# A hybrid decoder layer on one core: sine tables kept off other work, RG-LRU in finer steps and a later S5 scan, and smaller first transfers

## The chip, the cores and the metric

The kernel runs on one core of a Trainium2 chip. The core has a matrix engine (PE, with its weight loads as PEld), a vector engine (DVE), a scalar engine (ACT), a small general engine (POOL) and a sync engine (SP) that here issues nearly all transfers from memory. Each engine works through its own list of instructions in order and waits at semaphores for the others. The metric is device time in microseconds (us) of one execution; lower is better.

## The reference

One decoder layer on 256 tokens of width 2048, all in float32. The normed input is multiplied by one wide matrix; its columns feed three branches and three gates.

```python
xn = rms_norm(h, norm_mix_g)
proj = xn @ w_in                       # 2048 x 11264: u_s5, u_lru, q, k, v, gate_logits
gates = sigmoid(gate_logits + b_gate)
y_s5 = s5_branch(u_s5, ...)            # complex diagonal linear scan over time, gelu, glu
y_lru = rglru_branch(u_lru, ...)       # causal conv of 4 taps, two gates, real linear scan
y_attn = stick_breaking_attention(q, k, v)   # 8 heads, exp/log and a cumulative sum
merged = g_s5*(y_s5 @ w_br_s5) + g_lru*(y_lru @ w_br_lru) + g_attn*(y_attn @ w_br_attn)
h = h + merged @ w_out
h = h + squared_relu_mlp(rms_norm(h, norm_mlp_g), w_up, w_down)   # width 8192
return rms_norm(h, final_norm_g)
```

In the S5 branch the state turns by a fixed angle each step. The kernel takes the turning out before a real scan and puts it back after it, for which it needs, for each of eight blocks of channels, a table of cosines and sines of step times angle.

## The kernel before

**Weight units.** All large weights come in units of 256 x 512 values (512 KB), 520 of them, in one fixed list `stream`. Unit n passes through four hands. SP loads `raw_n` (`load_next`, L130). ACT casts it to a rounded half `hi_n` (`split_next`, L146). DVE subtracts, `lo_n` = `raw_n` - `hi_n` (L147). PE then multiplies: hi by the rounded activations, hi by their rest, and lo by the rounded ones, in three matmuls per tile, so that float32 is nearly kept. `chunk` (L225 to L227) does it with 24 matmuls of 128x256 per unit, `chunk_tok` (L241 to L243) with 12 of 128x512. raw, hi and lo have three buffers each: `hi_n` can be written only when PE has finished unit n-3, and `raw_n` is asked for only when `lo_(n-3)` is done.

**Units in order.** 0 to 15 give the RG-LRU input, 16 to 31 the S5 input. 32 to 79 are the RG-LRU gate and its branch product in turns of 8 and 4. 80 to 127 are k, q, v twice (four heads each time). 128 to 175 are the attention gate and branch in turns of 8 and 4 (gate: 128 to 135, 140 to 147, 152 to 159, 164 to 171), 176 to 191 the S5 gate's first half, and then come the S5 tail, the output product and the MLP.

**Side work.** Everything else (norm, RG-LRU, S5 scan, attention, gelu) is written as generators: pieces of work with `yield` between them. `later(gens, rate)` puts a generator in a list; after each unit's matmuls `pump` runs, on average, `rate` pieces of each generator in the list. So the rate and the number of yields say at which unit a piece is issued; then the framework's scheduler orders each engine's list. Side work on DVE and ACT thus stands between two lo's or two hi's, and whatever stands there delays the next one.

**The pieces that matter here.** `lru_half` runs the conv for a pair of channel tiles: one scaled copy on ACT (L535) and three multiply-adds on DVE (L537), then a yield; after that two sigmoid matmuls and sigmoids (L545, L546), Tanh, Exp, Sqrt, and a scan (L570) with the split of its result (L572, L573). It is queue `lq`, rate 1.15. The bank scalings of S5's input are L386. `s5_scan` (rate 1.27) starts as soon as its parameters are there: `s5_tables` makes a block's angles (L604), reduces them (L606, L607), takes Abs (L609) and two Sin on ACT (L610, L611), then `s5_split` and `s5_stack` build the scan's input with twelve 64 KB transfers on SP per block. Per block there follow six products on DVE (L660 to L670), eight scans (L705), six products (L681 to L692) and a sum into `us5` (L700). The next block's tables are stepped by hand between those products (`next(more, None)`). `gelu` has a Tanh, `gates` two multiply-adds on DVE (L750) and two Sigmoids on ACT (L751), `branch` the products with the gates (L760, or L762 and L763), `attention` per head Abs, Exp, Ln (L796 to L798), a suffix sum on PE and a last Exp (L811), all in a chain of seven steps. ACT holds one set of function tables at a time; where the set changes the list has an ACT_TABLE_LOAD.

**The start.** SP asks for x's tiles 0 and 1 in one transfer (256 KB), unit 0 in two, x's next pair, unit 1, and so on. The rounded x (`xhi`, L322) is made in `before_split` ahead of each unit's cast. Twenty small matmuls on ones keep PE busy from the start until the first unit is there.

Of the kernel before, what the change touches and what calls it, by code (L numbers as in the profile page):

```python
# [14 lines left out]
P = 128  # L15
L = 256
# [30 lines left out]
def hybrid_block(ctx: ExitStack, tc: tile.TileContext, io, out):  # L47
# [62 lines left out]
    st = {"load": 0, "split": 0, "use": 0}  # L110

    def pieces(i):
        return [slice(k, k + 1) for k in range(UK)] if i == 0 else [slice(0, UK)]

    def load_x(q):
        if q < KT // UK:
            s = slice(q * UK, q * UK + UK)
            nc.sync.dma_start(xT[:, s, :], io["x"][:, s, :])
        if q == 0:
            nc.scalar.dma_start(par, io["par"])  # L120

    def load_next():
# [6 lines left out]
        for k in pieces(i):  # L129
            nc.sync.dma_start(t[:, k, :], io[name][c * (ngrp[name] // (P * UK)) + g][:, k, :])  # L130
        raw[i] = t

    def split_next():
        i = st["split"]
        if i >= len(stream):
            return
        st["split"] += 1
        h = whi.tile([P, UK, CH], F32R, tag="hi", name=f"hi{i}")
        l_ = whi.tile([P, UK, CH], F32R, tag="lo", name=f"lo{i}")
        r = raw.pop(i)  # L140
        x = anchor.pop("x", None)
        es = ExitStack()
        if i == 0:
            es.enter_context(tc.issue_after(x))
        for k in pieces(i):
            anchor["act"] = nc.scalar.copy(h[:, k, :], r[:, k, :]).ins  # L146
            anchor["dve"] = nc.vector.tensor_tensor(l_[:, k, :], r[:, k, :], h[:, k, :].bitcast(F32), ALU.subtract).ins  # L147
        es.close()
        hi[i] = h, l_
# [82 lines left out]
    def chunk_tok(name, c, k, xs, hold=0, done=None):  # L232
# [12 lines left out]
        for g in range(ng - hold):  # L245
# [5 lines left out]
            anchor["pe"] = mm.ins  # L251
            pump()
# [47 lines left out]
    for q in range(3):  # L300
        load_next()
        load_x(q + 1)
# [220 lines left out]
    def lru_half(c, us):  # L523
# [9 lines left out]
        for u, cts, xc, r, i_, th in parts:  # L533
            for j, k in cts:
                nc.scalar.activation(xc[:, j, :], u[:, j, :], AF.Identity, scale=cw[:, 3, k], bias=cb[:, k])  # L535
                for s in range(1, 4):
                    nc.vector.scalar_tensor_tensor(xc[:, j, s:], u[:, j, :L - s], cw[:, 3 - s, k], xc[:, j, s:], ALU.mult, ALU.add)  # L537
                yield
# [37 lines left out]
    lq = later([lru_params()], 1.15)  # L576
# [16 lines left out]
    S5_RATE = 1.27  # L593

    def s5_tables(b):
# [7 lines left out]
        def gen():  # L603
            nc.vector.tensor_tensor(c, fhi[:, q, :].unsqueeze(3).broadcast_to(sh), flo[:, q, :].unsqueeze(2).broadcast_to(sh), ALU.add)  # L604
            yield
            nc.scalar.activation(sf, cf, AF.Identity, bias=magic)  # L606
            nc.vector.scalar_tensor_tensor(sf, sf, -MAGIC, cf, ALU.add, ALU.subtract)  # L607
            yield
            nc.scalar.activation(cf, sf, AF.Abs)  # L609
            nc.scalar.activation(sf, sf, AF.Sin, scale=-TURN)  # L610
# [20 lines left out]
    def s5_scan():  # L631
        v = ypool.tile([P, 2, NT, L], F32, tag="yhi", name="s5_v")
        t12 = ypool.tile([P, 2, NT, L], F32, tag="ylo", name="s5_t")
        vr, vi, t1, t2 = v[:, 0], v[:, 1], t12[:, 0], t12[:, 1]
        tabs, more = s5_tables(0)
        yield from more
        s5_split(0)
# [6 lines left out]
        for b in range(WT):  # L644
            c, s = tabs
# [9 lines left out]
            more = iter(())  # L655
            if b + 1 < WT:
                s5_split(b + 1)
                tabs, more = s5_tables(b + 1)
                yield
# [11 lines left out]
            next(more, None)  # L671
# [8 lines left out]
            next(more, None)  # L680
# [3 lines left out]
            next(more, None)  # L684
# [18 lines left out]

    def tt_scan(o, r, i):
        nc.vector.tensor_tensor_scan(o, r, i, 0.0, ALU.mult, ALU.add)  # L705

    def gelu(b):
# [4 lines left out]
        yield  # L712
        nc.scalar.activation(g1, g1, AF.Tanh, scale=GELU_C * GELU_K)
# [21 lines left out]
    def gates(idx, c, alloc):  # L735
# [9 lines left out]
        later([bias()], 1.0)  # L745
        banks = chunk_tok("w_in", GATE0 + 4 * idx + c, D, xs)
        gts = []
# [37 lines left out]
    def attention(hs, kT, qT, vt):  # L785
# [27 lines left out]
        tc.keep_in_program_order(nc.scalar.preload_act_table_set("natural_log_exp_and_others"))  # L813
        yield
        for i in range(7):
# [4 lines left out]
            yield  # L820
        while vt[0] is None:
            yield
# [348 lines left out]
```

## Time and profile before

| what | value |
| --- | --- |
| time, three runs | 1508.52, 1511.49, 1511.58 us; median 1511.49 |
| profiled execution, time | 1512.1 us |
| its span | 1510.3 us |
| PE busy | 1488.4 us, 99% |
| DVE busy | 1175.2 us, 78% |
| ACT busy | 782.3 us, 52% |
| transfers, mean | 194 GB/s |

How the lines are read: a line of a timeline gives the start, the length, the engine, the line of the kernel, the operation, what it writes and reads, how many are taken together, and in brackets how long the engine had been idle and what ended that. Lengths of neighbours on one engine overlap a little (a lo of 1.22 us is followed by the next start 1.13 later), so pitches are taken from starts. A row of the view by windows has, for a stretch of time, the busy time and number of instructions of PE, PEld, DVE, ACT and POOL, then the granted clock of PE (1.00 is full), the share of the transfer engines, and GB/s. Times are in us from the start of the profiled execution's span.

### The profile page before, as it was taken

Reading aid. Unit: us, or ns where it says so; the run is one execution under the profiler, and the core shown is the slowest. Engines: PE = TensorE matmul, PEld = TensorE weight load, DVE = VectorE, ACT = ScalarE, POOL = GpSimd, SP = SyncE. Lnnn points to the kernel's source line nnn. Section 1 sums busy time; section 2 is a strip of 40 time slices with the busy share of each in tenths; the row PEclk is TensorE's granted clock in tenths of the full one; section 3 lists DMA queues with packets and bytes.
Section 4 is the critical chain, followed back from the end, with each engine's and each line's share of the span. In section 5 each row is a group of like instructions: output and inputs, shape, how many; then the busy total and the mean of one; then the engine's idle time right before and its main releaser. Section 6 shows DMA issues by size and latency. Waiting matters only on the chain.

```text
span 1510.3 us, 19900 instructions
## 1 busy us (share of the span) xinstructions
PE 1488.4 (99%) x7518; PEld 1260.5 (83%) x7518; DVE 1175.2 (78%) x1468; ACT 782.3 (52%) x920; POOL 35.3 (2%) x60
## 2 busy tenths in 40 slices
PE   9999999999999999999999999999999999999997
PEld 9997788989887878988887888888888888888886
DVE  6767998897988989689799796568854787558965
ACT  6767556565765564544455544344433444344443
POOL 1400000000000000000000000000000000000011
PEclk9999999999999999999999999999999999999999
DMA  9546766665555666666855666666666666666664
GB/s 287 157 153 176 228 205 201 187 182 168 175 172 183 208 182 210 189 202 190 276 182 188 197 184 205 194 185 196 198 194 193 193 195 195 195 191 191 192 197 152
DMA packets 89858, 292.41 MB, mean 194 GB/s; under 512 B 12834, under 2 KB 17058, under 8 KB 89634
## 3 DMA queue, kind: packets, MB, share of 16 engines
q1 hardware_dynamic: 89618, 291.07, 62.6%
q8 instruction: 59, 0.97, 0.3%
q14 instruction: 37, 0.30, 0.1%
q10 hardware_dynamic: 144, 0.07, 0.0%
HBM read 282.71 MB, written 2.10 MB: 189 GB/s over the span
## 4 chain that ended last, share of the span: by engine, by line
PE 83%; DVE 9%; issue 3%; ACT 2%; DMA 2%; SPq 0%; DVEq 0%; ACTq 0%
PE mt_w_up L242 6%; PE mt_w_up L241 6%; PE mt_w_up L243 6%; PE mt_w_in L242 5%; PE mt_w_in L243 5%; PE mt_w_in L241 5%; PE mt_w_down L242 4%; PE mt_w_down L241 4%; PE mt_w_down L243 4%; PE mp_w_down L277 4%; PE mp_w_down L278 4%; PE mp_w_down L276 4%; PE mm_w_in L227 4%; PE mm_w_in L225 4%; PE mm_w_in L226 4%; DVE lo L147 3%
## 5 line engine op out<-in xcount | busy, mean ns | idle before, releaser
L146 ACT CAST hi<-raw 128x1024 fp32r<-128x1024 f32 (+1 forms) x521 | 545.2, 1049 | 625.9 <-PE mt_w_up L243 131.4
L147 DVE TENSOR_TENSOR lo<-raw,hi 128x1024 fp32r<-128x1024 f32 (+1 forms) x521 | 637.9, 1225 | 287.7 <-ACT hi L146 284.1
L242 PE MATMUL mt_w_in<-lo,xhi 128*128 128x512 f32 x448 | 176.1, 393 | 3.9 <-DVE lo L147 3.7
L241 PE MATMUL mt_w_in<-hi,xhi 128*128 128x512 f32 x448 | 175.2, 396 | 0.2 <-ACT hi L146 0.2
L243 PE MATMUL mt_w_in<-hi,xlo 128*128 128x512 f32 x448 | 175.2, 391 | 0.0
L241 PE MATMUL mt_w_up<-hi,hhi 128*128 128x512 f32 x448 | 174.3, 389 | 0.0
L242 PE MATMUL mt_w_up<-lo,hhi 128*128 128x512 f32 x448 | 174.3, 389 | 0.0
L243 PE MATMUL mt_w_up<-hi,hlo 128*128 128x512 f32 x448 | 174.3, 389 | 0.0
L227 PE MATMUL mm_w_in<-xhi,lo 128*128 128x256 f32 x512 | 145.4, 286 | 4.5 <-DVE lo L147 4.5
L225 PE MATMUL mm_w_in<-xhi,hi 128*128 128x256 f32 x512 | 146.5, 286 | 0.5 <-ACT hi L146 0.4
L226 PE MATMUL mm_w_in<-xlo,hi 128*128 128x256 f32 x512 | 145.7, 285 | 0.0
L728 DVE STREAM_TRANSPOSE reluT<-relu 32x256 f32<-32x256 f32 x256 | 111.5, 436 | 4.2
L242 PEld LDWEIGHTS mt_w_in<-lo,xhi 128*128 128x128 f32 x448 | 84.6, 189 | 24.0 <-DVE lo L147 7.6
L227 PEld LDWEIGHTS mm_w_in<-xhi,lo 128*128 128x128 f32 x512 | 98.7, 194 | 5.5 <-DVE lo L147 5.5
L242 PE MATMUL mt_w_down<-lo,hd_hi 128*128 128x512 f32 (+1 forms) x272 | 102.5, 377 | 0.0
L241 PE MATMUL mt_w_down<-hi,hd_hi 128*128 128x512 f32 (+1 forms) x272 | 102.4, 377 | 0.0
L243 PE MATMUL mt_w_down<-hi,hd_lo 128*128 128x512 f32 (+1 forms) x272 | 102.4, 376 | 0.0
L225 PEld LDWEIGHTS mm_w_in<-xhi,hi 128*128 128x128 f32 x512 | 99.2, 194 | 1.1 <-ACT hi L146 1.0
L277 PE MATMUL mp_w_down<-lo,hd_hi 128*128 128x512 f32 x256 | 99.8, 390 | 0.1
L278 PE MATMUL mp_w_down<-hi,hd_lo 128*128 128x512 f32 x256 | 99.6, 389 | 0.0
L276 PE MATMUL mp_w_down<-hi,hd_hi 128*128 128x512 f32 x256 | 99.6, 389 | 0.0
L241 PEld LDWEIGHTS mt_w_in<-hi,xhi 128*128 128x128 f32 x448 | 84.5, 189 | 17.8 <-ACT hi L146 0.7
(299 smaller groups left out, 2370.2 us busy)
## 6 DMA issues: line engine op xcount, KB each, us to landing
raw<-in_w_in SPq DMA_DIRECT2D x175, 512.0 KB, 4.3
raw<-in_w_up SPq DMA_DIRECT2D x128, 512.0 KB, 4.2
raw<-in_w_down SPq DMA_DIRECT2D x128, 512.0 KB, 4.2
raw<-in_w_out SPq DMA_DIRECT2D x32, 512.0 KB, 4.2
raw<-in_w_br_lru SPq DMA_DIRECT2D x16, 512.0 KB, 4.6
raw<-in_w_br_attn SPq DMA_DIRECT2D x16, 512.0 KB, 4.1
raw<-in_w_br_s SPq DMA_DIRECT2D x16, 512.0 KB, 4.1
stk<-ux SPq DMA_DIRECT2D x96, 64.0 KB, 4.1
```

Of the source, the lines that this page charges most:

```text
L146: anchor["act"] = nc.scalar.copy(h[:, k, :], r[:, k, :]).ins
L147: anchor["dve"] = nc.vector.tensor_tensor(l_[:, k, :], r[:, k, :], h[:, k, :].bitcast(F32), ALU.subtract).ins
L225: nc.tensor.matmul(o, wh[:, kk, s], xh, start=first and ct % 2 == 0, stop=False, skip_group_check=True)
L226: nc.tensor.matmul(o, wh[:, kk, s], xl, start=False, stop=False, skip_group_check=True)
L227: mm = nc.tensor.matmul(o, wl[:, kk, s], xh, start=False, stop=last and ct % 2 == 1, skip_group_check=True)
L241: nc.tensor.matmul(banks[j], xh[:, s], wh[:, a:b], start=kt == 0, stop=False)
L242: nc.tensor.matmul(banks[j], xh[:, s], wl[:, a:b], start=False, stop=False)
L243: return nc.tensor.matmul(banks[j], xl[:, s], wh[:, a:b], start=False, stop=kt == ng * UK - 1)
L276: nc.tensor.matmul(o, xh[:, s], wh[:, kk, :], start=kt == 0, stop=False)
L277: nc.tensor.matmul(o, xh[:, s], wl[:, kk, :], start=False, stop=False)
L278: mm = nc.tensor.matmul(o, xl[:, s], wh[:, kk, :], start=False, stop=kt == ng * UK - 1)
L728: nc.vector.transpose(d_[32 * a:32 * a + 32, :, :, 32 * b:32 * b + 32], s_[32 * b:32 * b + 32, :, :, 32 * a:32 * a + 32])
```

## The change

- **Start.** x's first pair is asked for in two transfers of 128 KB, and unit 0, in pieces of a quarter, a quarter and a half, is asked for between the two. Its casts and subtractions have the same pieces.
- **RG-LRU.** The conv yields inside each channel tile too (after the second multiply-add), and the queue's rate goes from 1.15 to 1.45.
- **S5 scan.** It yields eight times before its first table, and its rate goes from 1.27 to 1.35. The tables' generator has more yields and becomes a task of its own (`later([chain_of(3, more)], S5_RATE)`), finished at the latest when its block begins, in place of being stepped by hand.
- **Sines, gelu's Tanh.** The two Sin of a table wait (by yielding) while `st["chain"]` is set, that is while an attention's seven steps run, and while `st["gate"]` is set with fewer than three units of a gate product left. Gelu's Tanh waits for `chain`.

```diff
     def pieces(i):
-        return [slice(k, k + 1) for k in range(UK)] if i == 0 else [slice(0, UK)]
+        if i == 0:
+            return [(slice(0, 1), slice(0, L)), (slice(0, 1), slice(L, CH)), (slice(1, 2), slice(0, CH))]
+        return [(slice(0, UK), slice(0, CH))]
...
         if q < KT // UK:
-            s = slice(q * UK, q * UK + UK)
-            nc.sync.dma_start(xT[:, s, :], io["x"][:, s, :])
+            for s in ([slice(k, k + 1) for k in range(UK)] if q == 0 else [slice(q * UK, q * UK + UK)]):
+                nc.sync.dma_start(xT[:, s, :], io["x"][:, s, :])
+                if q == 0 and s.start == 0:
+                    load_next()
...
             anchor["pe"] = mm.ins
+            st["left"] = ng - 1 - g
             pump()
...
                 for s in range(1, 4):
                     nc.vector.scalar_tensor_tensor(xc[:, j, s:], u[:, j, :L - s], cw[:, 3 - s, k], xc[:, j, s:], ALU.mult, ALU.add)
+                    if s == 2:
+                        yield
                 yield
...
-    lq = later([lru_params()], 1.15)
+    lq = later([lru_params()], 1.45)
...
-    S5_RATE = 1.27
+    S5_RATE = 1.35
...
             nc.vector.tensor_tensor(c, fhi[:, q, :].unsqueeze(3).broadcast_to(sh), flo[:, q, :].unsqueeze(2).broadcast_to(sh), ALU.add)
             yield
+            yield
             nc.scalar.activation(sf, cf, AF.Identity, bias=magic)
             nc.vector.scalar_tensor_tensor(sf, sf, -MAGIC, cf, ALU.add, ALU.subtract)
             yield
+            yield
             nc.scalar.activation(cf, sf, AF.Abs)
+            yield
+            while st["chain"] or st["gate"] and st["left"] < 3:
+                yield
             nc.scalar.activation(sf, sf, AF.Sin, scale=-TURN)
             nc.scalar.activation(cf, cf, AF.Sin, scale=-TURN, bias=half_pi)
             yield
...
+        for _ in range(8):
+            yield
         tabs, more = s5_tables(0)
         yield from more
+        more = None
...
         for b in range(WT):
+            if more is not None:
+                finish(more)
...
                 tabs, more = s5_tables(b + 1)
+                more = later([chain_of(3, more)], S5_RATE)
                 yield
...
+    def chain_of(n, gen):
+        for _ in range(n):
+            yield
+        yield from gen
...
         yield
+        while st["chain"]:
+            yield
         nc.scalar.activation(g1, g1, AF.Tanh, scale=GELU_C * GELU_K)
...
+        st["gate"] = True
         banks = chunk_tok("w_in", GATE0 + 4 * idx + c, D, xs)
+        st["gate"] = False
...
+        st["chain"] = True
         yield
         for i in range(7):
...
+        st["chain"] = False
         while vt[0] is None:
             yield
```

Where instructions land is shown at three places. The first is DVE around unit 26 (before: L537 is the conv, L386 the scaling of a finished S5 bank, L573 the rest of the RG-LRU result; in the changed kernel the same are L543, L392 and L581). Before:

```order
L147 TENSOR_TENSOR lo25_1082<-raw25_1034,hi25_1081 128x1024
L573 TENSOR_TENSOR ylru_lo_151<-lru_tc0_631,ylru_hi_150 128x512
L537 SCALAR_TENSOR_TENSOR lru_xc1_1069<-ulru2_817,par_79,lru_xc1_1069 128x255 x2
L537 SCALAR_TENSOR_TENSOR lru_xc1_1069<-ulru2_817,par_79,lru_xc1_1069 128x254 x2
L537 SCALAR_TENSOR_TENSOR lru_xc1_1069<-ulru2_817,par_79,lru_xc1_1069 128x253 x2
L386 TENSOR_TENSOR us5_99<-mm_w_in_0_0_16_821,rstd_135 128x512
L386 TENSOR_TENSOR us5_99<-mm_w_in_0_1_16_822,rstd_135 128x512
L147 TENSOR_TENSOR lo26_1120<-raw26_1079,hi26_1119 128x1024
```

The same place in the changed kernel:

```order
L151 TENSOR_TENSOR lo25_1076<-raw25_1038,hi25_1075 128x1024
L581 TENSOR_TENSOR ylru_lo_153<-lru_tc0_635,ylru_hi_152 128x512
L543 SCALAR_TENSOR_TENSOR lru_xc1_1103<-ulru2_801,par_79,lru_xc1_1103 128x255
L392 TENSOR_TENSOR us5_101<-mm_w_in_0_0_16_805,rstd_137 128x512
L543 SCALAR_TENSOR_TENSOR lru_xc1_1103<-ulru2_801,par_79,lru_xc1_1103 128x254
L392 TENSOR_TENSOR us5_101<-mm_w_in_0_1_16_806,rstd_137 128x512
L151 TENSOR_TENSOR lo26_1119<-raw26_1073,hi26_1118 128x1024
L543 SCALAR_TENSOR_TENSOR lru_xc1_1103<-ulru2_801,par_79,lru_xc1_1103 128x253
```

Four of the six conv steps have moved behind lo26. At lo14 likewise one conv step stands ahead in place of six.

The second is ACT around unit 131, in the second attention (L811 and L835 are the last Exp of a head, z6 and z7 its scores; ts5 and tc5 are the sine and cosine table of S5's sixth block). Before:

```order
L146 CAST hi130_4172<-raw130_4138 128x1024
L606 ACTIVATE ts5_3854<-tc5_3853,magic_133 128x1024
L811 ACTIVATE z7_4075<-z7_4075 128x384
L146 CAST hi131_4194<-raw131_4170 128x1024
L609 ACTIVATE tc5_3853<-ts5_3854 128x1024
L610 ACT_TABLE_LOAD
L610 ACTIVATE ts5_3854<-ts5_3854 128x1024
L611 ACTIVATE tc5_3853<-tc5_3853,half_pi_131 128x1024
L146 CAST hi132_4216<-raw132_4192 128x1024
```

In the changed kernel:

```order
L150 CAST hi130_4176<-raw130_4139 128x1024
L835 ACTIVATE z6_4025<-z6_4025 128x384
L623 ACT_TABLE_LOAD
L623 ACTIVATE ts5_3940<-ts5_3940 128x1024
L835 ACT_TABLE_LOAD
L835 ACTIVATE z7_4063<-z7_4063 128x384
L624 ACT_TABLE_LOAD
L624 ACTIVATE tc5_3939<-tc5_3939,half_pi_133 128x1024
L150 CAST hi131_4197<-raw131_4174 128x1024
L150 CAST hi132_4217<-raw132_4195 128x1024
```

The sines have moved from between hi131 and hi132 to between hi130 and hi131, with z7's Exp between them. At unit 151 it is the other way: before, the gate's table load and two Sigmoids stood between the two Sin of ts6 and tc6, and now the Sin stand ahead of hi147 and the Sigmoids alone ahead of hi151.

The third is SP at the start. Before:

```order
L118 DMA xT_81<-in_x 128x512
L130 DMA raw0_86<-in_w_in 128x512 x2
L118 DMA xT_81<-in_x 128x512
L130 DMA raw1_90<-in_w_in 128x1024
L118 DMA xT_81<-in_x 128x512
L130 DMA raw2_93<-in_w_in 128x1024
```

In the changed kernel:

```order
L120 DMA xT_81<-in_x 128x256
L134 DMA raw0_85<-in_w_in 128x256 x2
L134 DMA raw0_85<-in_w_in 128x512
L120 DMA xT_81<-in_x 128x256
L120 DMA xT_81<-in_x 128x512
L134 DMA raw1_92<-in_w_in 128x1024
L120 DMA xT_81<-in_x 128x512
L134 DMA raw2_95<-in_w_in 128x1024
```

x's second tile has moved behind all of unit 0, and raw1 from fifth to seventh place. On ACT the two casts of xhi still stand together ahead of the first piece of hi0.

More of the change, by code (lines that the diff above doesn't have):

```diff
@@ L109, in hybrid_block @@
     raw, hi, anchor = {}, {}, {}
-    st = {"load": 0, "split": 0, "use": 0}
+    st = {"load": 0, "split": 0, "use": 0, "gate": False, "left": 0, "chain": False}
     def pieces(i):
-        return [slice(k, k + 1) for k in range(UK)] if i == 0 else [slice(0, UK)]
+        if i == 0:
+            return [(slice(0, 1), slice(0, L)), (slice(0, 1), slice(L, CH)), (slice(1, 2), slice(0, CH))]
+        return [(slice(0, UK), slice(0, CH))]
     def load_x(q):
         if q < KT // UK:
-            s = slice(q * UK, q * UK + UK)
-            nc.sync.dma_start(xT[:, s, :], io["x"][:, s, :])
+            for s in ([slice(k, k + 1) for k in range(UK)] if q == 0 else [slice(q * UK, q * UK + UK)]):
+                nc.sync.dma_start(xT[:, s, :], io["x"][:, s, :])
+                if q == 0 and s.start == 0:
+                    load_next()
         if q == 0:
@@ L128, in load_next @@
         t = wraw.tile([P, UK, CH], F32, tag="raw", name=f"raw{i}")
-        for k in pieces(i):
-            nc.sync.dma_start(t[:, k, :], io[name][c * (ngrp[name] // (P * UK)) + g][:, k, :])
+        for k, m in pieces(i):
+            nc.sync.dma_start(t[:, k, m], io[name][c * (ngrp[name] // (P * UK)) + g][:, k, m])
         raw[i] = t
@@ L144, in split_next @@
             es.enter_context(tc.issue_after(x))
-        for k in pieces(i):
-            anchor["act"] = nc.scalar.copy(h[:, k, :], r[:, k, :]).ins
-            anchor["dve"] = nc.vector.tensor_tensor(l_[:, k, :], r[:, k, :], h[:, k, :].bitcast(F32), ALU.subtract).ins
+        for k, m in pieces(i):
+            anchor["act"] = nc.scalar.copy(h[:, k, m], r[:, k, m]).ins
+            anchor["dve"] = nc.vector.tensor_tensor(l_[:, k, m], r[:, k, m], h[:, k, m].bitcast(F32), ALU.subtract).ins
         es.close()
@@ L300, in hybrid_block @@
     for q in range(3):
-        load_next()
+        if q:
+            load_next()
         load_x(q + 1)
@@ L654, in s5_scan @@
                     yield
-            more = iter(())
             if b + 1 < WT:
@@ L670, in s5_scan @@
             tt(t3, t3, vr, ALU.subtract)
-            next(more, None)
             yield
@@ L679, in s5_scan @@
                     yield
-            next(more, None)
             tt(t2, t1, c, ALU.mult)
@@ L683, in s5_scan @@
             tt(vr, t3, s, ALU.mult)
-            next(more, None)
             yield
```

## The prediction

> **What bounds the kernel now.** The page comes first: the matrix engine is busy for all but 22 us of the span, so only what makes it late can move the end.
>
> ```profile
> PE 1488.4 (99%) x7518; PEld 1260.5 (83%) x7518; DVE 1175.2 (78%) x1468; ACT 782.3 (52%) x920; POOL 35.3 (2%) x60
> ```
>
> The view of waits, asked for PE from 44 to 55, from 80 to 135, from 135 to 200 and from 450 to 545 us, says what it is late for (total, times, longest).
>
> ```profile
> PE mm_w_in L227 <- DVE lo L147: 1.8, 2, 1.3
> ...
> PE mt_w_in L242 <- DVE lo L147: 2.9, 3, 1.9
> PE mm_w_in L227 <- DVE lo L147: 2.2, 2, 1.9
> ...
> PE mt_w_in L242 <- DVE lo L147: 0.4, 1, 0.4
> ...
> PE mt_w_br_attn L241 <- ACT hi L146: 2.2, 1, 2.2
> PE mt_w_in L242 <- DVE lo L147: 0.4, 1, 0.4
> PE mt_w_in L241 <- ACT hi L146: 0.2, 1, 0.2
> ```
>
> It waits for weight halves, and never for the scan, the gates or attention themselves. Three stretches of PE's timeline show the pitch, unit 131's first matmul and the longest gap: 0.12 us for a 128x256 matmul (24 make a unit, 2.88), 0.23 for a 128x512 (12 make 2.72).
>
> ```profile
> 89.98 0.28 PE L225 MATMUL mm_w_in<-xhi,hi 128*128 128x256 f32 x1
> 90.10 0.28 PE L226 MATMUL mm_w_in<-xlo,hi 128*128 128x256 f32 x1
> ...
> 422.21 0.48 PE L241 MATMUL mt_w_in<-hi,xhi 128*128 128x512 f32 x1
> ...
> 481.31 0.39 PE L242 MATMUL mt_w_br_attn<-lo,ya_hi 128*128 128x512 f32 x1
> 481.54 0.39 PE L243 MATMUL mt_w_br_attn<-hi,ya_lo 128*128 128x512 f32 x1
> 484.08 0.73 PE L241 MATMUL mt_w_br_attn<-hi,ya_hi 128*128 128x512 f32 x2 [2.15 <-ACT hi L146]
> ```
>
> By starts, that gap costs 484.08 - 481.54 - 0.23 = 2.3: a gap and about 0.15 more. Then there is an aftermath. The view by windows, in steps of 3.41 us (span, PE busy first, granted clock third from the end):
>
> ```profile
> 44.73:48.14 3.41, 2.08 (x18) 1.88 (x16) 3.38 (x8) 2.82 (x5) 2.19 (x6) 1.00 0.01 2
> 89.11:92.52 3.41, 1.48 (x12) 1.28 (x11) 3.41 (x7) 1.33 (x2) 0.00 (x0) 1.00 0.20 82
> 92.52:95.93 3.41, 3.41 (x17) 3.41 (x17) 3.41 (x7) 0.00 (x0) 0.00 (x0) 0.50 0.73 180
> 130.07:133.48 3.41, 3.41 (x10) 2.64 (x9) 2.82 (x6) 3.40 (x5) 0.00 (x0) 0.50 0.64 190
> 481.64:485.05 3.41, 1.04 (x5) 0.32 (x3) 0.99 (x1) 3.40 (x5) 0.00 (x0) 1.00 0.08 26
> 485.05:488.46 3.41, 3.41 (x8) 2.74 (x9) 3.41 (x4) 0.87 (x1) 0.00 (x0) 0.50 0.51 154
> ```
>
> There are three such half windows, behind the three waits of 1.9 to 2.2 us. After a window with PE busy for 1.04 or 1.48 us the next one runs at half clock and loses 3.41 x 0.5 = 1.7 us of matmuls; after one with 2.08 it does not. So a gap near 2 us inside one window costs 3.7. The Trainium skill, "TensorE: Matmul & The Clock Gate", "Why this matters for your kernels", allows idle gaps up to about 3 us; by it none of the three gaps should have halved the clock, and the measurement decides.
>
> **Part 1, RG-LRU and the later scan: +6.9.** Before, in DVE's timeline:
>
> ```profile
> 48.00 2.44 DVE L537 SCALAR_TENSOR_TENSOR lru_xc<-ulru,par,lru_xc 128x255 f32<-128x255 f32 x6
> ...
> 87.47 2.45 DVE L537 SCALAR_TENSOR_TENSOR lru_xc<-ulru,par,lru_xc 128x255 f32<-128x255 f32 x6
> 89.84 1.29 DVE L386 TENSOR_TENSOR us<-mm_w_in,rstd 128x512 f32<-128x512 f32 x2
> 91.04 1.22 DVE L147 TENSOR_TENSOR lo<-raw,hi 128x1024 fp32r<-128x1024 f32 x1
> ```
>
> Six conv steps stand ahead of lo14 and lo26. What goes: unit 14's wait, 0.5 of PE's 1.8 us in that stretch, with its restart 0.65; from 80 to 135 us 2.9 + 2.2 of waits, five restarts of 0.15, and two half windows of 1.7, together 9.3. Sum 9.9. What comes: the change leaves two conv steps and two bank scalings ahead of lo26 instead of six and two, but the gate products and two scans that stood before units 23 and 24 now crowd into unit 24. At the starts above (1.13 a lo, 0.60 a 512-wide operation, 0.40 a conv step) units 24, 25 and 26 take 4.1, 3.5 and 3.7 on DVE against 3 x 2.88 of matmuls: 2.7 late, less some 0.5 in hand (lo23 ended 0.3 before unit 23's first matmul, and lo is needed 0.24 after it), 2.2 in three pieces, the longest about 0.9, so no half window. The two table-loading ACT blocks move from units 31 and 32 to 33 and 34: I leave them 0.6, and 0.2 for the late scans at unit 38. The scan's first sine table leaves units 35 to 38, where lo36 stood behind it. 9.9 - 2.2 - 0.6 - 0.2 = 6.9. Bounds: 9.9 if the new pieces hide; 5 if the conv's pieces at unit 26 still make one half window.
>
> **Part 2, units 50 to 60: -1.9.** The scan's first products now run there with the gates. For units 52 to 58 DVE has 3.5, 2.4, 5.1, 3.6, 2.4, 3.7 and 3.2 us against 2.72 each (unit 54: two 128x1024 products of 1.22, two gate operations of some 0.7, lo 1.2): 4.9 too much by recorded lengths, some 4.2 by starts, which come 0.08 sooner per operation. The halves are at most about 2.9 ahead, since only three buffers of each exist. On top, twelve stacking transfers stand in a row on SP between raw49 and raw50, which uses up that lead. The nearest row is unit 142:
>
> ```profile
> 450.98 1.22 DVE L666 TENSOR_TENSOR t<-s_v,tc 128x1024 f32<-128x1024 f32 x1
> ...
> 455.65 1.22 DVE L147 TENSOR_TENSOR lo<-raw,hi 128x1024 fp32r<-128x1024 f32 x1
> ```
>
> Two products, the gates and the sums, 4.7 us from 450.98 on, stand ahead of one lo; with the lead full they cost only the two small waits of 450 to 545 us (0.6). So: 0.5 with full lead, 4.2 with none; I take 2.5, nearer the upper middle as the transfers sit just ahead, less the 0.6 that 135 to 200 us has now (0.4 and a restart).
>
> **Part 3, sines against gates and attention: +0.1.** ACT's timeline before, around unit 151 and around hi130:
>
> ```profile
> 473.81 1.06 ACT L146 CAST hi<-raw 128x1024 fp32r<-128x1024 f32 x1 [0.49 <-PE mt_w_in L243]
> ...
> 477.13 1.06 ACT L610 ACTIVATE ts<-ts 128x1024 f32<-128x1024 f32 x1
> 478.20 1.28 ACT L751 ACT_TABLE_LOAD   x1
> ...
> 480.65 1.28 ACT L611 ACT_TABLE_LOAD   x1
> 481.95 1.15 ACT L611 ACTIVATE tc<-tc,half_pi 128x1024 f32<-128x1024 f32 x1
> 483.00 2.92 ACT L146 CAST hi<-raw 128x1024 fp32r<-128x1024 f32 x3
> ...
> 412.68 0.51 ACT L811 ACTIVATE z<-z 128x384 f32<-128x384 f32 x1
> 413.09 0.68 ACT L849 ACTIVATE vt<-mt_w_in,rstd_tok 128x512 f32<-128x512 f32 x1
> 413.66 1.04 ACT L146 CAST hi<-raw 128x1024 fp32r<-128x1024 f32 x1
> ```
>
> The sigmoids cut between the two sines: three table loads, 9.2 us from hi to hi. The change parts them, so unit 151 falls to 3.6 us on ACT. With its half window, 450 to 545 us is 2.8 of waits + 3 x 0.15 + 1.7 = 5.0, which goes. But the order shows the same cut made anew: after hi130 come Exp(z6), a table, a sine, a table, Exp(z7), a table, the other sine. hi130 follows the value copies, which wait for PE as before, and so ends near 414.6 (the starts above, one cast 0.95 behind another); then by these rows 0.45 + 1.29 + 1.06 + 1.29 + 0.5 + 1.29 + 1.05 = 6.9 until hi131 may start, 421.5; it ends at 422.5 and lo131 at 423.8. Unit 131 started at 422.21, and two matmuls on hi now stand ahead of the first on lo: 0.3 late, then 0.9 more, with the restart 1.3. A window then holds about 2.1 us of busy PE, the value of the row at 44.73 that kept its clock: I give a half window one chance in five, 1.6 in all (1.3 to 3.9 with what may be late ahead of it). Behind it on ACT only hi132 queues. Further: both sines at unit 147 and the gate products at 142 and 143, 1.0; unit 154, where 5.8 us on DVE end with lo154, 1.3 (0.6 by unit 142, 2.6 without lead); unit 165, 1.0. Sum 4.9 (2 to 9). Table loads stay 33 of 33, so nothing is saved in their number. ScalarE's row of 1.28, with the next instruction 0.01 behind it, is what I price. The Trainium skill, "ScalarE: Activation LUTs", "What ACT_TABLE_LOAD costs", adds a drain of 1.38, by which the three loads at unit 131 would cost some 4 more (an estimate); the rows above show no drain.
>
> **Part 4, the start: -0.4.**
>
> ```profile
> 1.04 4.64 PE L329 MATMUL warm<-ones 128*128 128x128 f32 x20 [1.04 <-POOL eps_t L338]
> 6.05 0.58 PE L225 MATMUL mm_w_in<-xhi,hi 128*128 128x256 f32 x1 [0.37 <-ACT hi L146]
> ...
> 6.48 0.62 ACT L146 CAST hi<-raw 128x512 fp32r<-128x512 f32 x1 [0.49 <-DMA raw<-in_w_in]
> 8.70 1.05 ACT L146 CAST hi<-raw 128x1024 fp32r<-128x1024 f32 x1 [0.38 <-DMA raw<-in_w_in]
> ...
> 9.78 1.23 DVE L147 TENSOR_TENSOR lo<-raw,hi 128x1024 fp32r<-128x1024 f32 x1 [0.94 <-ACT hi L146]
> ```
>
> x's second tile is now queued behind all of raw0, and ACT does both xhi before hi0. 768 KB lie ahead of and in it, as many as up to raw0's second half, which landed by 6.48: the first matmul moves from 6.05 to about 7.5. Unit 0 ends at 10.4. But PE was bound by lo1 (11.0): hi1, behind xhi and hi0 pieces, ends near 10.1 rather than 9.74, so 0.4 late. The idle stretch from 5.68 leaves 1.91 us busy in the window up to 7.19, between 1.48 and 2.08: if the clock stays half, unit 0 ends at 11.9 and the loss is 1.4. No gain: bytes ahead of raw1 are unchanged.
>
> **The sum.** 6.9 - 1.9 + 0.1 - 0.4 = +4.7. The profiled execution took 1512.1 (span 1510.3), so 1507.4; it lies 0.6 above the median, 1511.5, so **1506.8**. After unit 186 both orders agree, and the scan still ends before finish(sq) asks for it: 0.
>
> **Rivals.** (a) The new crowding hides under the lead, as unit 142's did: 9.9 + 0.6 + 5.0 - (0.6 + 0.5 + 2.0 + 0.4) = 12, so 1499.5. For it: the leads; against it: the transfers ahead of raw50. (b) The stalls only change place: part 1 gives 5, part 2 costs 3.6, part 3 1.5 (6.5 at its bounds without a half window, against 5.0), the start 0.4: -0.5, so 1512. For it: the order at unit 131, where the sines, moved off the gates, meet the exponentials that they were to keep off too: there the change does not do what it says. (c) Slower, by one mechanism, the half clock: it decides once a window holds under some 1.5 to 2.0 us of busy PE. If the new stalls around units 26, 54, 131 and 154 and the start all tip it, that is 4 x 1.7 + 1.0 - 0.3 (already counted) and 0.8 of further idle time each at 54 and 154 to get there, 9.1 more than the forecast: 1515.9. Against it: by the rows only a wait near 1.9 us does it, and I find none that long.
>
> **Numbers.** Forecast 0.44 (own range 1503.5 to 1510.5), (a) 0.22, (b) 0.21, (c) 0.13. A measurement tells 0.2%, 3 us, from no change. Faster by more: (a) and four fifths of the forecast, 0.57; slower: most of (c), 0.12; same: 0.31. The range, from (a) to the near side of (c): 1499 to 1514.
>
> **What would show it.** Right: no wait over 1 us between 80 and 135 us and no half clock there; at unit 131 a wait of some 1.2 us for hi and lo; none at unit 151; the first real matmul past 7 us. Wrong: half clock in the window after 7.19, waits over 3 us in units 52 to 60, or no wait at unit 131.

## The result, and the profile after

The changed kernel took 1514.59 us (median of 9 executions, 1511.97 to 1516.06), the kernel before 1511.31 (9 executions, 1508.52 to 1512.33). The ratio is 1.0021, with a 95% interval of 1.0012 to 1.0030: slower by 0.2%, about 3.2 us, where 4.7 us less was forecast. That is 0.6 us above the upper end of the range that was given. Two executions of the experiments below (1640.09 us in e6 and 1552.85 in e7) ran in a slower state, at mean clocks of 0.849 and 0.901; the ratios leave them out, the medians of e6 and e7 include them.

The profiled execution of the changed kernel took 1511.97 us, as good as the 1512.1 of before. That is the first thing to explain: one was the fastest execution of its kernel, the other near the slowest of its own.

The page of the changed kernel:

```profile
span 1510.2 us, 19908 instructions
PE 1485.6 (98%) x7518; PEld 1257.0 (83%) x7518; DVE 1176.0 (78%) x1469; ACT 782.9 (52%) x921; POOL 35.4 (2%) x60
```

Its waits of PE over the whole span (total, times, longest):

```profile
PE mt_w_in L246 <- DVE lo L151: 5.6, 8, 2.5
PE mm_w_in L231 <- DVE lo L151: 3.7, 5, 1.6
PE mm_w_in L229 <- ACT hi L150: 1.7, 1, 1.7
PE mt_w_in L245 <- ACT hi L150: 1.4, 1, 1.4
PE mt_w_br_lru L246 <- DVE lo L151: 1.1, 1, 1.1
```

With two small ones, 0.9 at mp_w_up and 0.2 at mt_w_out, these sum to 14.6 us, the wait ahead of the warm-up left out. The same view of before sums to 11.9 us. So there is more waiting, not less, and yet the profiled spans are equal. What differs the other way is the clock. The view by windows, on the grid of 3.41 us that this execution's clock records have:

```profile
5.01:8.43 3.42, 1.68 (x14) 1.48 (x13) 1.58 (x4) 2.13 (x6) 0.69 (x1) 1.00 0.84 276
8.43:11.84 3.41, 3.41 (x19) 3.41 (x18) 2.73 (x6) 2.47 (x5) 0.00 (x0) 0.50 1.03 386
45.97:49.39 3.42, 1.85 (x16) 1.65 (x15) 3.35 (x9) 3.28 (x6) 1.48 (x3) 1.00 0.01 2
...
489.70:493.12 3.42, 1.82 (x8) 1.14 (x7) 3.42 (x6) 1.35 (x2) 0.00 (x0) 1.00 0.33 131
493.12:496.53 3.41, 2.55 (x14) 1.85 (x18) 3.41 (x4) 0.00 (x0) 0.00 (x0) 1.00 0.43 123
```

One half window, behind the new idle stretch at the start (1.68 us of busy PE). Two others came near: 1.85 and 1.82 us of busy PE kept the clock, though the wait at 491 us was 2.5 us long, because a border of the grid cut it. The execution of before had three half windows; this one had one.

The gaps themselves came where the order put them. Around unit 131, ACT's timeline, and PE's (L835 is the Exp of z6 and then z7, L623 and L624 the two Sin, L150 the casts hi131 and hi132):

```profile
413.93 0.53 ACT L835 ACTIVATE z<-z 128x384 f32<-128x384 f32 x1 [0.67 <-DVE z L834]
414.46 1.28 ACT L623 ACT_TABLE_LOAD   x1
415.75 1.06 ACT L623 ACTIVATE ts<-ts 128x1024 f32<-128x1024 f32 x1
416.82 1.28 ACT L835 ACT_TABLE_LOAD   x1
418.12 0.53 ACT L835 ACTIVATE z<-z 128x384 f32<-128x384 f32 x1
418.65 1.28 ACT L624 ACT_TABLE_LOAD   x1
419.94 1.15 ACT L624 ACTIVATE tc<-tc,half_pi 128x1024 f32<-128x1024 f32 x1
421.00 1.98 ACT L150 CAST hi<-raw 128x1024 fp32r<-128x1024 f32 x2
...
422.07 0.73 PE L245 MATMUL mt_w_in<-hi,xhi 128*128 128x512 f32 x2 [1.41 <-ACT hi L150]
423.33 0.50 PE L246 MATMUL mt_w_in<-lo,xhi 128*128 128x512 f32 x1 [0.53 <-DVE lo L151]
```

Exp(z6) itself waited 0.67 us for DVE, then three table loads stand ahead of hi131: PE waits 1.4 us for hi, 0.5 for lo. At unit 154 DVE shows the crowd: six operations stand between lo153 (486.89) and lo154, the row at 492.71. The two rows of ACT are hi153 and hi154.

```profile
488.04 1.22 DVE L703 TENSOR_TENSOR s_v<-t,tc 128x1024 f32<-128x1024 f32 x1
489.17 1.22 DVE L705 TENSOR_TENSOR s_t<-s_t,ts 128x1024 f32<-128x1024 f32 x1
490.31 1.28 DVE L786 TENSOR_TENSOR gate<-mt_w_br_attn,gate 128x512 f32<-128x512 f32 x2
491.51 1.28 DVE L787 TENSOR_TENSOR merged<-merged,gate 128x512 f32<-128x512 f32 x2
492.71 1.22 DVE L151 TENSOR_TENSOR lo<-raw,hi 128x1024 fp32r<-128x1024 f32 x1
...
485.81 1.05 ACT L150 CAST hi<-raw 128x1024 fp32r<-128x1024 f32 x1 [3.76 <-DMA raw<-in_w_in]
487.08 1.05 ACT L150 CAST hi<-raw 128x1024 fp32r<-128x1024 f32 x1 [0.22 <-DMA raw<-in_w_in]
```

Both casts waited for their transfers, but hi154 was done at 488.14, 4.6 us before lo154 began, so it was DVE's list that held unit 154. The transfers hung on DVE too: SP asked for raw152, raw153 and raw154 each 0.03 us after lo149, lo150 and lo151 (476.36, 479.39, 481.81) had freed their buffers. From 455 to 495 us DVE was busy for 37.1 of 40 us, before for 34.0.

At the start PE was idle for 1.74 us:

```profile
1.04 4.38 PE L335 MATMUL warm<-ones 128*128 128x128 f32 x20 [1.04 <-POOL eps_t L344]
7.16 0.39 PE L229 MATMUL mm_w_in<-xhi,hi 128*128 128x256 f32 x1 [1.74 <-ACT hi L150]
```

### The profile page after: what moved, and what is told of

It is laid out like the page before. It is cut to its first block, busy times and chain, and to the rows that moved or that the text cites. A ratio compares the mean times of both kernels' runs of the same rounds, so it can differ in the third digit from the quotient of the medians.

```text
span 1510.2 us, 19908 instructions
## 1 busy us (share of the span) xinstructions
PE 1485.6 (98%) x7518; PEld 1257.0 (83%) x7518; DVE 1176.0 (78%) x1469; ACT 782.9 (52%) x921; POOL 35.4 (2%) x60
## 4 chain that ended last, share of the span: by engine, by line
PE 72%; DVE 15%; ACT 5%; issue 4%; DMA 3%; SPq 0%; DVEq 0%; ACTq 0%
PE mt_w_up L247 6%; PE mt_w_up L246 6%; PE mt_w_up L245 6%; DVE lo L151 6%; PE mt_w_in L246 4%; PE mt_w_in L247 4%; PE mt_w_in L245 4%; PE mt_w_down L245 4%; PE mt_w_down L246 4%; PE mt_w_down L247 4%; PE mp_w_down L282 4%; PE mp_w_down L283 4%; PE mp_w_down L281 4%; PE mm_w_in L231 3%; PE mm_w_in L229 3%
## 5 line engine op out<-in xcount | busy, mean ns | idle before, releaser
L150 ACT CAST hi<-raw 128x1024 fp32r<-128x1024 f32 (+1 forms) x522 | 545.3, 1048 | 624.3 <-PE mt_w_up L247 131.1
```

Of the source, the lines that this page charges most:

```text
L150: anchor["act"] = nc.scalar.copy(h[:, k, m], r[:, k, m]).ins
```

## The experiments

Two theories stood against each other in most of them. A: what counts is which piece of side work stands ahead of which lo or hi, the clock behind a gap is halved or not by chance, and the start costs more than was forecast. B, in several shapes: the start costs nothing, or waits only change their place. All were run beside the kernel before, in three sets: e1 to e4, e5 to e8, e9 to e12. Its median was 1510.55, 1510.43 and 1509.77 us there. Times of different sets are compared by their ratios to it.

### The kernel before once more: how much is chance

No edit.

> The kernel before, unchanged, to see its granted clock execution by execution. Theory A (half-clock lottery): a window of 3.41 us runs at half clock only when the PE was idle for more than half of the window before it, and where the borders of the windows fall differs from execution to execution; then the mean clock of an execution moves in steps of about 0.0011 (3.41 x 0.5 / 1510), its span by about 1.7 us a step, over zero to three steps for the three gaps near 2 us, a spread of 3 to 5 us. Rival B (no lottery): the executions differ by less than 1 us at one clock, or their time does not go with the clock.

Measured (e1): 1509.96 us, ratio 0.9998 (0.9989 to 1.0007). Over the 70 executions of the kernel before in the first two sets the time goes with the mean granted clock:

```
mean clock   executions   mean time
0.995            10        1511.7
0.996            31        1510.8
0.997            15        1509.8
0.998            11        1509.1
0.999             3        1509.3
```

The straight line through them falls by 0.79 us per 0.001. One half window is 3.41 x 0.5 / 1510 = 0.0011 of clock, so by this line it is worth about 0.9 us, not the 1.7 that it takes. The line is a low estimate, since the mean clock holds something more: in every profile the last 3.4 to 6.5 us of the span, behind PE's last matmul, stand at 0.50 too. That takes 0.0011 to 0.0022 from the mean, depending on where the borders fall, and holds up no matmul.

The profile of this run has no half window behind any gap (clock 0.999) and took 1509.1 us. The gaps are there, at units 26 and 151:

```profile
90.88:94.29 3.41, 2.10 (x17) 2.10 (x18) 3.41 (x6) 0.65 (x1) 0.00 (x0) 1.00 0.27 83
479.99:483.41 3.42, 2.01 (x8) 1.36 (x9) 2.25 (x2) 3.04 (x4) 0.00 (x0) 1.00 0.05 4
```

The waits in them are 1.93 and 2.15 us, as in the profiled execution of before, where these windows held 1.48 and 1.04 us of busy PE and were followed by half clock. Here the borders fall elsewhere and cut the same gaps. Its waits are longer in sum:

```profile
PE mm_w_in L227 <- DVE lo L147: 4.5, 4, 1.9
PE mt_w_in L242 <- DVE lo L147: 3.5, 7, 1.3
PE mt_w_br_attn L241 <- ACT hi L146: 2.2, 1, 2.2
```

With five smaller ones (0.9 at mp_w_up, 0.8 and 0.6 at hi, 0.6 at mt_w_out, 0.2 at mt_w_br_lru) these are 13.3 us, against 11.9 in the execution with three half windows: while PE is slow, the halves can get ahead, and later waits shrink (PE waits 0.4 us at unit 38 and 0.2 at 153 here, and not at all there, where half windows came just before). The two profiled executions differ by 1512.1 - 1509.1 = 3.0 us, 1.0 for each of the three windows. Theory A holds, with a smaller price: about 1 us.

### The first transfers alone

```diff
 the kernel before, with
+            return [(slice(0, 1), slice(0, L)), (slice(0, 1), slice(L, CH)), (slice(1, 2), slice(0, CH))]
...
+                if q == 0 and s.start == 0:
+                    load_next()
```

> Only the first transfers are changed (x's first pair in two, unit 0 in three pieces and between them). Theory A: the first real matmul comes about 1.1 us later, unit 0 runs a window at half clock in about half of the executions, and lo1 does not hide it: 1.5 to 3 us slower than before. Rival B: lo1 was the bound before and stays it, as the prediction had it: 0.4 us slower, not to be told from no change.

Measured (e2): 1512.17 us, ratio 1.0011 (1.0002 to 1.0020), 1.6 us slower. Its windows:

```profile
3.91:7.32 3.41, 1.11 (x10) 0.92 (x9) 0.93 (x3) 1.12 (x4) 1.81 (x1) 1.00 0.75 263
7.32:10.74 3.42, 3.42 (x17) 3.42 (x18) 2.17 (x6) 2.44 (x6) 0.00 (x0) 0.50 0.99 339
```

The first real matmul came at 7.19 us, against 6.05 before, and then at half clock. The price lies near the upper bound that was given for it (1.4), though the interval alone (0.3 to 3.0 us) does not exclude the 0.4 that was forecast.

What is lost can be read where the start is over, at the first matmul of unit 12. It came at 42.66 to 43.71 us (mean 43.1) in the nine profiles with the first transfers of before, and at 44.23 to 44.71 (mean 44.4) in the five with the changed ones, 1.3 us later. SP's requests for raw1, before and here in the changed kernel:

```profile
2.65 0.44 SPq L130 DMA_DIRECT2D raw<-in_w_in  x1
...
3.60 0.43 SPq L134 DMA_DIRECT2D raw<-in_w_in  x1
```

Each request takes SP some 0.47 us, and raw1 now stands two places later. hi1 ended at 9.2 to 9.7 us in the nine and at 10.1 to 11.3 in the five.

### The first transfers alone, with more warm-up

```diff
 as the last one, with
-WARM = 10
+WARM = 14
```

> Only the first transfers are changed (as in e2), with 14 pairs of warm-up matmuls in place of 10, so that PE is busy until about the time that the first real matmul can start. Theory A: part of e2's 1.6 us is the half clock behind an idle window; with no idle stretch no window at half clock follows, 0.5 to 1.2 us of the 1.6 go, and the first real matmul starts no earlier. Rival B: e2's loss is the later data alone: the same time as e2 (1.6 us slower than before).

Measured (e6): 1511.09 us, ratio 1.0006 (0.9997 to 1.0015), 0.7 slower than before. The warm-up's last matmul ended near 6.5 us, the first real one came at 7.40, and the windows around it had 3.13 and 2.80 us of busy PE and full clock. So the half window went. That time went with it is not shown: the intervals of e2 and e6 overlap, and the profiles speak against it. Unit 12 began at 44.71 us here, at 44.26 in e2 with its half window. With full clock PE waits for hi1 instead (0.68 us at 11.30), which ended at 11.25. Theory B, that the later data alone set the start's price, fits these two profiles better.

### The changed kernel without its first transfers

```diff
 the changed kernel, with pieces, load_x, load_next and the first loads as in the kernel before
```

> The changed kernel with the first transfers as they were before. Theory A: the start held most of the loss, so 0 to 1.5 us slower than before (1511 to 1512.5). Rival B: the loss sits in the new waits of units 50 to 60 and 131 to 165, so still about 3 us slower (1514).

Measured (e3): 1511.16 us, ratio 1.0007 (0.9998 to 1.0016). Without the start the change is not to be told from no change. The start makes the difference between 1.0007 and 1.0021; on the kernel before it made 1.0011. The sum of the two parts, 1.0018, agrees with the whole.

### The RG-LRU part alone

```diff
 the kernel before, with
+                    if s == 2:
+                        yield
...
-    lq = later([lru_params()], 1.15)
+    lq = later([lru_params()], 1.45)
```

> Only the RG-LRU part: the conv yields inside each channel tile and its queue runs at 1.45; the S5 scan, the sines and the start as before. Theory A: the waits at units 14, 26 and 32 shrink (2.1 to 0.9 us at 26), and with unit 26's gap goes one place that can halve the clock, while the scan's first table now meets the RG-LRU scans at units 35 to 38 (4.7, 3.5, 2.3 and 4.4 us on DVE): 1 to 3 us faster than before. Rival B (stalls only change place): the waits at 24 to 26 and 35 to 38 add up to what unit 26 and 36 cost before: within 0.7 us of before.

Measured (e4): 1510.44 us, ratio 0.9998 (0.9989 to 1.0007): nothing gained. Rival B holds here. Between 80 and 135 us its PE waits are

```profile
PE mt_w_in L242 <- DVE lo L147: 3.2, 4, 1.7
PE mm_w_in L227 <- DVE lo L147: 1.9, 3, 0.7
```

With one of 0.9 for a hi these are 6.0 us, against 5.1 before. The 1.9 us at unit 26 became three waits of 0.6 to 0.7, as forecast; but the RG-LRU's last products now met the scan's first table, and DVE had 3.5 us of work ahead of lo35 at 118 to 121 us, where PE then waited 1.7. Its executions lost about one half window less (mean clock 0.9976 against 0.9965), which pays for the longer waits.

### The scan and the sines alone

```diff
 the kernel before, with the scan's eight yields, its rate 1.35, the tables' task and the flags, but the RG-LRU as it was
```

> Only the S5 scan's delay, its tables' own task and the waits of the sines are changed; the RG-LRU and the start are as before. Theory A: the RG-LRU's gain and this part's loss add up to e3: the waits at units 14 and 26 stay (26 with its chance of a half window), units 35 to 38 are freed, units 54 to 57, 131 and 154 get theirs: 1 to 3 us slower than before (1511.5 to 1513.5). Rival B: this part is what gains, by the parted gates and sines, and the RG-LRU's rate is what loses: 1 us faster than before.

Measured (e7): 1511.73 us, ratio 1.0010 (1.0001 to 1.0019). The wait of 1.9 at unit 26 is there again, units 35 to 38 are free, and at unit 131 PE waits 1.4 and 0.5 as in the changed kernel. Theory A's number (1 to 3 us slower) holds. Neither part is worth anything alone; together they are worth about what they are worth apart.

### Keeping the sines out of the second attention

```diff
 the changed kernel without its first transfers, with
+        for _ in range(2):
+            yield
         st["chain"] = False
```

> The changed kernel with the first transfers as before (as in e3) and one thing more: the attention's flag is cleared two steps later, so that no sine can be put between the last two Exp of the second attention. Theory A: the wait at unit 131 (1.4 for hi and 0.5 for lo in the profiles) was caused by the sines cutting the exponentials apart; it goes, 2 to 3 us faster than e3, 1 to 2.5 us faster than before. Rival B: the sines' time comes back one unit later (a new wait of like size at units 132 to 135), so the same as e3.

Measured (e5): 1506.83 us, ratio 0.9979 (0.9970 to 0.9989): 3.6 us faster than before, 4.2 faster by the ratios than without these two yields (e3). In the changed kernel the flag fell one pump after the piece with the last Exp was issued, and the scheduler put the ready sine ahead of an Exp that still waited for DVE. ACT's timeline now:

```profile
412.62 0.53 ACT L830 ACTIVATE z<-z 128x384 f32<-128x384 f32 x1 [0.98 <-DVE z L829]
...
415.62 1.28 ACT L618 ACT_TABLE_LOAD   x1
416.91 1.06 ACT L618 ACTIVATE ts<-ts 128x1024 f32<-128x1024 f32 x1
417.88 1.14 ACT L619 ACTIVATE tc<-tc,half_pi 128x1024 f32<-128x1024 f32 x1
418.92 1.03 ACT L146 CAST hi<-raw 128x1024 fp32r<-128x1024 f32 x1
```

Two table loads fewer and no wait of PE at all between 405 and 450 us; rival B, that the time comes back a unit later, falls. The profiled executions of e3 and e5 differ by 2.7 us (1508.85 and 1506.13, both without a half window), of which the two waits and their restarts are 2.2. The mean clock of all its executions rose from 0.9971 to 0.9981, about one half window less, 0.9 by the line above. The rest is within the intervals.

### Other numbers: fewer long waits

```diff
 as the last one, with
-    lq = later([lru_params()], 1.45)
+    lq = later([lru_params()], 1.6)
-    S5_RATE = 1.35
+    S5_RATE = 1.33
-            while st["chain"] or st["gate"] and st["left"] < 3:
+            while st["chain"] or st["gate"] and st["left"] < 2:
-        for _ in range(8):
+        for _ in range(5):
-                more = later([chain_of(3, more)], S5_RATE)
+                more = later([chain_of(4, more)], S5_RATE)
         rsqrt_mean(rstd_tok, ps[:, L:L + 2], 2)
+        yield
         lru_in(0)
```

> The same means with other numbers and the start as before: RG-LRU rate 1.6, five yields before the scan's first table in place of eight, scan rate 1.33, the sines wait only for the last two units of a gate, the tables' task starts four steps later, the attention's flag is cleared two steps later, and the RG-LRU's first scaling stands one step behind the norm's (which frees lo13). Theory A (what counts is only which piece stands ahead of which lo or hi): with 1.5 us as the longest wait no gap can halve the clock, and the waits add up to some 5 us less than before: 3 to 7 us faster (1504 to 1508). Rival B (a wait only changes its place whatever the numbers): within 1 us of before.

Measured (e8): 1505.99 us, ratio 0.9968 (0.9955 to 0.9980). In its profile no wait over 1.3 us is left, and there is no half window. That is inside theory A's range; no edit of the six was run alone.

### Smaller pieces: the best version

```diff
 against the last one
-    lq = later([lru_params()], 1.6)
+    lq = later([lru_params()], 1.75)
-        for _ in range(5):
+        for _ in range(6):
-                more = later([chain_of(4, more)], S5_RATE)
+                more = later([chain_of(3, more)], S5_RATE)
+        yield
         rsqrt_mean(rstd_tok, ps[:, L:L + 2], 2)
-        yield
         lru_in(0)
             nc.vector.tensor_tensor(i_, i_, th, ALU.mult)
-        yield
+            yield
                 nc.vector.tensor_tensor_scan(xc[:, j, :], r[:, j, :], i_[:, j, :], 0.0, ALU.mult, ALU.add)
+                yield
```

> As e8, but numbers chosen so that no unit of the first 200 has more than about its own length on DVE or ACT ahead of its lo or hi: RG-LRU rate 1.75 with a yield more after each product and each scan, six yields before the scan's first table, scan rate 1.33, sines kept off the last two units of a gate, tables' task three steps later, attention's flag cleared two steps later, and the first token scalings one step later; the start as before. Theory A (waits do not move if the pieces are small enough): no wait over 1.5 us, none between 12 and 140 us, and some 11 us less waiting than before: 8 to 13 us faster (1498 to 1502). Rival B (the waits are conserved, or half windows repay themselves): no better than e8's 1506.

Measured (e9): 1500.81 us, ratio 0.9939 (0.9926 to 0.9953): 9 us faster than before, some 12 faster by the ratios than the changed kernel. Its waits over the whole span:

```profile
PE mt_w_in L242 <- DVE lo L147: 3.5, 5, 1.9
PE mm_w_in L225 <- ACT hi L146: 1.1, 2, 0.9
PE mp_w_up L278 <- DVE lo L147: 0.9, 1, 0.9
PE mt_w_br_lru L242 <- DVE lo L147: 0.8, 1, 0.8
PE mm_w_in L227 <- DVE lo L147: 0.5, 1, 0.5
```

6.8 us, against 14.6 in the changed kernel and 11.9 or 13.3 before, and none between 12 and 135 us. The theory that waits are conserved falls. That they are conserved only while the pieces are as large as the lead fits, and is not shown by itself. Theory A's time came out, but not its sum: it expected some 11 us less waiting, and 5 to 6.5 went. With a restart of 0.15 for each wait that is gone, and 0.6 for the clock (mean 0.9978 against 0.9971 of the kernel before in the same set), this leaves an estimated 1 to 2.5 us of the 9 that no view here explains. DVE at units 26 and 27 (the two lo), where six conv steps, two scalings and a product once stood ahead of lo26 alone:

```profile
85.08 1.26 DVE L388 TENSOR_TENSOR us<-mm_w_in,rstd 128x512 f32<-128x512 f32 x2
86.26 1.21 DVE L147 TENSOR_TENSOR lo<-raw,hi 128x1024 fp32r<-128x1024 f32 x1
87.39 0.68 DVE L578 TENSOR_TENSOR ylru_lo<-lru_tc,ylru_hi 128x512 fp32r<-128x512 f32 x1
87.99 0.48 DVE L539 SCALAR_TENSOR_TENSOR lru_xc<-ulru,par,lru_xc 128x255 f32<-128x255 f32 x1
88.39 1.22 DVE L147 TENSOR_TENSOR lo<-raw,hi 128x1024 fp32r<-128x1024 f32 x1
```

One wait is, against the expectation, still there: 1.9 us for lo154 in the attention gates (479 to 481 us), where 1.5 at most was expected.

### The best version without the rule for gates

```diff
 as the last one, with
-            while st["chain"] or st["gate"] and st["left"] < 2:
+            while st["chain"] or st["gate"] and st["left"] < 0:
-    S5_RATE = 1.33
+    S5_RATE = 1.31
-                more = later([chain_of(3, more)], S5_RATE)
+                more = later([chain_of(2, more)], S5_RATE)
```

and the yield of the RG-LRU's products and that of the norm back where e8 has them.

> As e9 with the sines not kept off the gates at all (the condition on a gate's last units never holds), scan rate 1.31 and the tables' task two steps later. Theory A (what counts is where the pieces fall; the rule for gates is one way among others to set that): within 1.5 us of e9. Rival B (the rule for gates is what takes the wait at unit 151 away): a wait of about 2 us at a gate comes back, 2 to 4 us slower than e9.

Measured (e10): 1502.09 us, ratio 0.9950 (0.9938 to 0.9963). Within 1.3 us of e9, and the intervals overlap. No wait at unit 151 came back, and that at unit 154 is 1.8 us, much as in e9. So the rule that keeps sines off the gates is not needed for this time. What it alone is worth is not shown, since the other numbers were moved with it.

### The best version with the changed first transfers

```diff
 the best version, with the first transfers of the changed kernel
```

> As e9 with the changed first transfers. Theory A: their price stands alone here, 1.1 us of later first matmul, the more by what the clock adds: 1 to 2.5 us slower than e9. Rival B: 0.4 us (lo1 is the bound either way).

Measured (e11): 1500.71 us, ratio 0.9946 (0.9933 to 0.9959), against 0.9939: no difference that five executions can tell. Three of them had clock 0.999 and took 1500.3 to 1500.7, two had 0.997 and 0.996 and took 1503.0 and 1504.2; their mean is 1501.7, e9's 1500.7. The profiled execution, at 0.999, begins unit 12 at 44.41 us, e9's at 43.20. So the start is 1.2 us later here too, with full clock, and the 1 to 2.5 us of theory A are neither confirmed nor excluded.

### The changed kernel, mended

```diff
 the changed kernel, with
+        for _ in range(2):
+            yield
         st["chain"] = False
...
-WARM = 10
+WARM = 14
```

> The changed kernel, all of it, with two lines mended: the attention's flag is cleared two steps later, and there are 14 pairs of warm-up matmuls. Theory A: 4 us go by the first (e5 against e3) and about 1 by the second (e6 against e2): 1509 to 1510.5, 1 us faster than before or the same. Rival B (the start's price is not the clock's, and cannot be mended so): 1511.5 or more.

Measured (e12): 1509.01 us, ratio 0.9992 (0.9984 to 1.0001). The two edits together take 0.29% out of the changed kernel, 4.4 us. e5 against e3 is 0.28%, so the attention's flag accounts for it within the intervals, and nothing is left to show for the warm-up.

## Why the prediction was wrong

**The step that failed is the sum's price of the clock.** The sum was made against one execution, and took that execution's three half windows as the kernel's own: 2 x 1.7 in part 1 and 1.7 in part 3, 5.1 us of gain, with 0.3 for new ones. Without these terms the four parts come to 3.5 - 1.9 - 1.3 - 0.4 = -0.1, so the whole forecast gain of 4.7 us was the clock. The runs show two things in its place. First, a half window comes or not by where the grid's border cuts a gap: the same waits at units 26 and 151 had it in one execution of the kernel before and not in another. The kernel before lost on average as much clock (mean 0.9965) as the changed one (0.9963). With 0.0016, the mean over the fourteen profiles, taken off for the end of the span, that is an estimated 1.7 and 1.9 half windows per execution, where the sum had 3 and 0.2. Second, a window is worth about 1 us (0.9 by the line, 1.0 by the two profiles) and not 1.7, since part of it comes back in shorter waits. So the net 4.8 us of clock were not there to be had from this change, whose new gaps at the start, at 131 and at 154 are of like length to those it removed. The step "it lies 0.6 above the median" saw the sign of this and not its cause.

With the clock at nothing, the parts as measured below come to 3.1 - 3.1 - 2.9 - 1.3 = -4.2 us, against -3.2 in the result (1.8 to 4.5 slower).

**Part 1 was right in its waits.** Without half windows it was 9.9 - 3.4 = 6.5 of stalls that go and 3.0 that come. After: 0.9, 0.75 and 0.75 at units 24 to 26, each with the restart counted, 0.7 at 34 and 0.3 at 38, 3.4 in all, and unit 14's wait is gone. That the RG-LRU alone gains nothing, and the later scan is needed for it, was in the prediction only by the sentence on the scan's first table.

**Part 2 had the right mechanism and was short in size:** 2.5 forecast, 3.0 measured (0.8, 1.2, 0.5, 0.4), though the first of these came at unit 48, ahead of the stretch that it named. And 0.7 more came at 250 and 262 us, which was not foreseen. Less the 0.6 that went, it is 3.1.

**Part 3 was right in place and short in size.** Unit 131: 1.3 without the clock forecast, 2.2 measured. From hi130's end to hi131's start it took 7.7 us in place of the 6.9 that were added up, mainly since Exp(z6) waited 0.67 for DVE. Unit 154: 1.3 forecast, 2.6 measured, the bound given for no lead. There was no lead because DVE itself had none to spare, as the rows at 488 to 493 us show. lo154 did begin earlier than before (492.71 us against 494.41), but PE was there earlier still. Together with the small ones 6.2 instead of 4.6 us, against 3.3 that went, both without the clock. Unit 151's wait did go.

**Part 4 had the first matmul right and raw1 wrong.** It came past 7 us, as forecast. The 0.4 was hi1's delay behind the pieces on ACT, with raw1 taken to land as before since the bytes ahead of it are unchanged. But raw1 is asked for at 3.60 us in place of 2.65, behind two more requests. In the changed kernel's own profile hi1 still ended at 10.1 us, as forecast, and there it is the half clock, the case for which the bound of 1.4 was given, that makes unit 0 end late (1.68 us of busy PE, as the warm-up ended at 5.4 and not 5.7 us). In the other four profiles hi1 ended at 10.8 to 11.3, and the three of them without a half window at the start are no earlier at unit 12. So either is enough for a loss near 1.3 us. That the later request is what makes raw1 late fits these profiles and was not tested by itself.

**The signs.** All four signs of being right came (no wait over 1 us and no half clock from 80 to 135 us; the wait at 131, 1.9 us for the 1.2 named; none at 151; the first matmul past 7 us), and one of the three of being wrong, the half clock at the start. They were signs of the waits. None of them asked how much clock the kernel before loses on average.

**Rivals.** (c), the half clock, gave 1515.9 and was nearest to 1514.6. That is luck in the number: its mechanism, more half windows than before, is not what made the changed kernel slower, as the mean clocks show. Nor is it one tipping point, but a draw for each gap in each execution. (b) came next, at 1512, and its mechanism is nearer: the waits that went at units 26, 36 and 151 came back at the start, 54, 131 and 154. e4 is (b) in pure form. (a) was out of reach of this change, and nearly reached by the best version (1500.8 against 1499.5), which needed smaller pieces than the change made.

## What to carry to other kernels

Before an execution's stalls are priced, look at how its clock stands among the other executions: what is chance in it is not to be gained by an edit that leaves gaps of like length. When a transfer is moved in a list of requests, look at every one that it pushes back, and not only at the bytes. In a stream that one engine must never starve, the piece of side work between two feeds has to stay under the lead that the buffers allow; splitting pieces pays only when all that lands near them is split too, since the waits move to the next crowded feed. A flag that is to keep work apart must outlast the instructions it protects, not the point where they are issued.

## What was not expected of the hardware

The first profile's rows (half clock behind 1.04 and 1.48 us of busy PE, none behind 2.08) can be set against all fourteen profiles, with windows of 3.41 us on each execution's own grid. Between the clock's first record and PE's last matmul, all six windows with 1.04 to 1.32 us of busy PE were followed by half clock. All with 1.77 or more were followed by full clock. Between them, from 1.48 to 1.70, seven were followed by half clock (1.48 to 1.68) and four by full: 1.49 in e3, 1.56 in e10, 1.62 in e5 and 1.70 in e11. So the border lies near half of the window, but busy time as the profile has it does not decide every case. A misplaced grid is not the reason, as the clock's first record and its last, 1.5 ms later, fit one grid to 0.01 us in each profile. PE's ends are modelled; whether that is the reason stays open.

The profile of e7 shows the wait at unit 154 again, here with the border where it tips:

```profile
488.65:492.06 3.41, 1.61 (x8) 1.03 (x7) 3.41 (x6) 1.05 (x1) 0.00 (x0) 1.00 0.04 18
492.06:495.48 3.42, 3.42 (x9) 2.65 (x10) 3.19 (x3) 0.00 (x0) 0.00 (x0) 0.50 0.53 182
```

And a half window's 1.7 us of lost matmuls cost about 1 us of time in the kernel before, since later waits were shorter.
